# A one-core float32 transformer and recurrent block whose SBUF layout moves: a smaller GpSimd scratch, nine staging buffers in attention, fillers ahead of the column operands

## The chip, the cores and the metric

One core of a Trainium2 chip. The metric is device microseconds of one execution. The kernel before was timed three times: 881.23, 882.3 and 886.79 us, median 882.3 us. On 1 % of that, 8.8 us, rest the words faster, same and slower below.

## The reference

Two layers on one sequence of T = 256 tokens, D = 1024, everything float32 (cut):

```python
def first_block(x, mem, positions, ...):
    h = rms_norm(x, attn_norm_g)
    proj = h @ w_in                      # split into c_q, c_kv, k_pe, rq, rk, rv, rg
    a_out = mla_group(...)               # causal attention, 4 heads
    r_out = retention_group(...)         # chunked retention, 4 heads
    x = x + concat([a_out, r_out]) @ w_out
    x = x + memory_cross_attention(rms_norm(x, ...), rms_norm(mem, ...), ...)
    return x + hierarchical_moe(rms_norm(x, ...), ...)   # 32 experts, top 2

def hybrid_layer(x, p_i, ...):
    z = rmsnorm(x, g_mix) @ w_in         # 7 parts: RNN, convolutions, gates
    ...
    x = x + merged @ w_out
    g, u = split(rmsnorm(x, g_ffn) @ w_gate_up)
    x = x + (silu(g) * u) @ w_down
    return x + sigmoid(rmsnorm(x, g_ple) @ w_ple_gate) * (p_i @ w_ple)
```

## The kernel before, in words

All weights lie in one long array in the order of use, cut into chunks of mostly 128 x 2048 float32 (1 MB). `Stream.load` fetches them on one DMA queue of SyncE (L171), always in that order. There are three families: the A chunks (attention and cross attention), 96 M chunks for the experts (eight groups of four experts, in each eight gate/up chunks and four down chunks; they are numbered 0 to 95 here), and the B chunks (second layer).

**Columns.** Outside the experts a matrix product is done in columns: `dense_w` (L239) makes one 128x256 result from blocks of 128x128. For float32 accuracy a weight piece of 128x512 is first split: `wh` is a rounded copy of it (ScalarE, L195) and `wl` the remainder (VectorE, L196); an activation has likewise a high part and a low part (`hh` and `ll`; `ch`/`cl` and `moh`/`mol` in attention, `ach`/`acl`, `xch`/`xcl`, `pth`/`ptl` in cross attention). Each block then costs three matmuls of 256 columns: `wh` by high, `wh` by low, `wl` by high. `lead` (L249) does the same for several columns at once. `wh` and `wl` have four buffers up to the experts and eight after (WBUF_A, WBUF_B).

**Experts.** A chunk is used raw as moving operand (L1017 gate/up, L1068 down), and its buffer is free when TensorE has read it. While attention and cross attention still compute, M chunks are fetched ahead into whatever tiles are idle. Which one takes which chunk is written down by `_plan` from the list ORDER: three tiles "r", seven "rx" (RINGX), "ll" and "hh" (a ring of two each), four "w", "ck", "cv", two "rz" (RINGZ) and one "xs", 23 in all. So chunks 0 to 22 go out before the experts begin and chunk 23 takes the tile of chunk 0, and so on round. Each load waits on its tile alone, but the queue is strictly in order: an issue that waits holds up all that follow. In the last group fewer kinds of tiles are allowed, as those of the second layer take their place.

At group 4 (chunk 48) the program has a branch (L951, for experts with too many tokens; its body isn't run with these inputs). The tile "rz" is left out of the plan for the chunks before it, and its pool is released and opened again there.

**Second layer.** After the last group's scatter (L1054) the columns begin again at L239 with the B chunks in "w" and "r" tiles. They go on to the end.

**Addresses.** Every tile has a fixed place in each of the 128 partitions of SBUF; pools are stacked in the order of their allocation on top of the GpSimd scratch, and pools with side="right" grow from the other end. No operation of the kernel names an address; they follow from the sizes of what is allocated before.

Of the kernel before, what the change touches and what calls it, by code (L numbers as in the profile page):

```python
# [9 lines left out]
F32 = mybir.dt.float32  # L10
F32R = mybir.dt.float32r
I32 = mybir.dt.int32
BF16 = mybir.dt.bfloat16
# [5 lines left out]
P = 128  # L19
T = 256  # L20
D = 1024
KT = 8
EPS = 1e-6
NEG = -1e30
NE = 32
# [6 lines left out]
CHUNK = 2048  # L32
RING1 = 4
RING2 = 3
RINGX = 7
RINGZ = 2
WARM = 16
WBUF_A = 4
WBUF_B = 8
AHEAD = 3  # L40
# [68 lines left out]
def block_kernel(tc, wst, cst_d, csa_d, sml_d, rw_d, dec_d, xt_d, pt_d, pos_d, out_d, dbg=None):  # L109
    nc = tc.nc  # L110
    V, S, TE = nc.vector, nc.scalar, nc.tensor

    glob = tc.alloc_tile_pool(name="glob", bufs=1)
    smp = tc.alloc_tile_pool(name="smp", bufs=2)
    xsp = tc.alloc_tile_pool(name="xsp", bufs=1)
    hlp = tc.alloc_tile_pool(name="hlp", bufs=2)
    psd = tc.alloc_tile_pool(name="psd", bufs=4, space=PSUM)
    psa = tc.alloc_tile_pool(name="psa", bufs=3, space=PSUM)
    pss = tc.alloc_tile_pool(name="pss", bufs=1, space=PSUM)
    ring1 = tc.alloc_tile_pool(name="ring1", bufs=RING1)  # L120
    crs = tc.alloc_tile_pool(name="crs", bufs=1)
    wsp = tc.alloc_tile_pool(name="wsp", bufs=WBUF_A)

# [16 lines left out]

    ident, ones = C("ident"), C("ones")
    ltb = glob.tile([P, P], BF16, name="ltb")
    oneb = glob.tile([P, P], BF16, name="oneb")


    class Stream:
# [71 lines left out]
    ws = Stream()  # L218
# [146 lines left out]
    nc.sync.dma_start(x0[:, 4:8], xt_d[:, 4:8])  # L365
    ws.load(4)
    nc.sync.dma_start(cst, cst_d)
    csa = wsp.tile([P, NCSA], F32, name="csa", bufs=1)
    nc.sync.dma_start(csa, csa_d)
    nc.sync.dma_start(sml, sml_d)  # L370
    posi = rtmp.tile([P, T], I32, name="posi")
    nc.sync.dma_start(posi, pos_d)
# [23 lines left out]
    ch = mla.tile([P, 3, T], F32R, name="ch")  # L396
    cl = mla.tile([P, 3, T], F32R, name="cl")
    csq = rtmp.tile([P, 3, T], F32, name="csq")
    qsq = mla.tile([P, 6, T], F32, name="s6")
    ksq = mla.tile([P, 5, T], F32, name="s5")  # L400
    kpe = mla.tile([P, T], F32, name="kpe")
# [143 lines left out]
    V.tensor_copy(ltb, C("lt"))  # L545
    V.memset(oneb, 1.0)

    moh = mla.tile([P, KT, T], F32R, name="moh")
    mol = mla.tile([P, KT, T], F32R, name="mol")


    def softmax_pt(ps, nk, f, pool, ptd):
        mx = smp.tile([P, 1], F32, name="mx")
# [70 lines left out]

    bns = mla.tile([P, 8, 6], F32, name="bns")
    bna = mla.tile([P, 8, 2], F32, name="bna")
    ro = mla.tile([P, 8, P], F32, name="s6")

    def retention(h):
# [186 lines left out]
        V.tensor_mul(m.rearrange("p t (g e) -> p (t g) e", g=4), o, gsb)  # L816

    rps = psa.tile([P, 3, NE], F32, name="a")
    for i, mats in enumerate(((ltb,), (oneb, ltb), (oneb, oneb))):
        for j, mat in enumerate(mats):  # L820
            for k in range(2):
                TE.matmul(rps[:, i], mat, msk[k][:, j], start=j == 0 and k == 0, stop=j == len(mats) - 1 and k == 1)
# [89 lines left out]
    V.tensor_copy(gate[:, :, :, 4:5], r2[:, :, None, None].to_broadcast([P, 2, NGRP, 1]))  # L912

    lam = G("lam", 0, 8)
    na = smp.tile([P, 8], F32, name="na")
    with tc.issue_after(ins1.ins):
        V.tensor_scalar(na, lam, -1.0, None, op0=OP.mult)
    V.tensor_tensor(na, na, lam, op=OP.min)
    ee = smp.tile([P, 8], F32, name="ee")
    S.activation(ee, na, AF.Exp)  # L920
    den = smp.tile([P, 8], F32, name="den")
    V.tensor_scalar(den, ee, 2.0, None, op0=OP.add)
    V.reciprocal(den, den)
    s1 = smp.tile([P, 8], F32, name="s1")
    V.tensor_mul(s1, ee, den)
    s2 = smp.tile([P, 8], F32, name="s2")
    V.tensor_mul(s2, s1, s1)
    hq = smp.tile([P, 8], F32, name="hq")
    V.memset(hq, 1.0 / 19)
    for k in (17, 15, 13, 11, 9, 7, 5, 3, 1):  # L930
        V.tensor_mul(hq, hq, s2)
# [1 line left out]
    V.tensor_mul(hq, hq, s1)  # L933
    sp8 = glob.tile([P, 8], F32, name="sp8")
    spn = glob.tile([P, 8], F32, name="spn")
    mn = smp.tile([P, 8], F32, name="mn")
    with tc.issue_after(ins1.ins):
        V.tensor_scalar(mn, lam, -1.0, 0.0, op0=OP.mult, op1=OP.max)
    V.scalar_tensor_tensor(sp8, hq, 2.0, mn, op0=OP.mult, op1=OP.add)
# [6 lines left out]
    def overflow():  # L946

        n_it = nc.values_load(ntrip[0:1, 0:1], min_val=0, max_val=NGRP)
        wexp = wst[OFFS[NA]:OFFS[NA + NM]].rearrange("(g c p f) -> g c p f", g=NGRP, c=12, p=P)
        lpp = tc.alloc_tile_pool(name="lpp", bufs=1, side="right")  # L950
        with tc.If(n_it > 0):  # L951
            with tc.For_i(0, n_it, 1) as gi:
                gres = lpp.tile([P, 2, NE], F32, name="gres")
                V.tensor_scalar(gres, rank, float(CAP - RBASE), None, op0=OP.is_ge)
                for tt in range(2):
                    gv = gres[:, tt].rearrange("p (g e) -> p g e", g=NGRP)
                    V.tensor_mul(gv, gv, gate[:, tt, :, 0:4])
                    V.tensor_scalar(gres[:, tt], gres[:, tt], r2[:, tt:tt + 1], None, op0=OP.mult)
                xg = lpp.tile([P, KT, T], F32, name="lxg")
                for kt in range(KT):  # L960
                    pt = small()
                    for tt in range(2):
                        TE.transpose(pt[:, tt], xt[:, tt, kt * P:(kt + 1) * P], ident)
                    V.tensor_copy(xg[:, kt].rearrange("p (t c) -> p t c", t=2), pt)
                for q in range(4):
                    pg = [bank() for _ in range(2)]
                    for kt in range(KT):
                        w = lpp.tile([P, 512], F32, name="lw", bufs=2)
                        nc.gpsimd.dma_start(w, wexp[bass.ds(gi, 1), kt, :, q * 512:(q + 1) * 512]
                                          .rearrange("a p f -> p (a f)"))  # L970
                        for tt in range(2):
                            TE.matmul(pg[tt], xg[:, kt, tt * P:(tt + 1) * P], w, start=kt == 0, stop=kt == KT - 1)
                    at = lpp.tile([P, 2, T], F32, name="lat")
                    for tt in range(2):
                        a = lpp.tile([P, T], F32, name="la")
                        S.activation(a, pg[tt][:, 0:T], AF.Silu, scale=r2[:, tt:tt + 1])
                        V.scalar_tensor_tensor(a, pg[tt][:, T:512], gres[:, tt, bass.ds(gi * 4 + q, 1)], a,
                                               op0=OP.mult, op1=OP.mult)
                        pt = small()
                        for f in range(2):  # L980
                            TE.transpose(pt[:, f], a[:, f * P:(f + 1) * P], ident)
                        V.tensor_copy(at[:, :, tt * P:(tt + 1) * P], pt)
                    for hf in range(2):
                        wd = []
                        for f in range(2):
                            w = lpp.tile([P, 512], F32, name="lw", bufs=2)
                            nc.gpsimd.dma_start(w, wexp[bass.ds(gi, 1), 8 + 2 * hf + f, :, q * 512:(q + 1) * 512]
                                              .rearrange("a p f -> p (a f)"))
                            wd.append(w)
                        for m in range(4):  # L990
                            for f in range(2):
                                TE.matmul(acc[4 * hf + m], wd[f][:, m * P:(m + 1) * P], at[:, f], start=False, stop=False,
                                          skip_group_check=True)
        lpp.release()
# [332 lines left out]
            eng = nc.sync if m % 4 == 0 else nc.scalar  # L1327
            eng.dma_start(out_d[:, a:m + 1], x6[:, a:m + 1])

    for pool in (ft, fp, wsp, ws.pools["r2"], pss, psa, psd, ring1, hlp, xsp, smp, glob):  # L1330
        pool.release()


# [199 lines left out]
```

## Time and profile before

| what | before |
|---|---|
| median of 3 runs | 882.3 us (881.23 to 886.79) |
| profiled execution, its own time | 881.19 us |
| its span | 879.5 us |
| granted TensorE clock over the span | 0.987 |
| TensorE busy | 834.5 us, 95 % |
| VectorE busy | 558.1 us, 63 % |
| ScalarE busy | 460.5 us, 52 % |
| weights read | 212.70 MB, 243 GB/s over the span |

The profiled execution lies 1.1 us below the median. Of its 881.19 us, 1.7 us lie around the span. The page's busy time of a matmul counts from its start to a modelled end, and neighbours overlap in it; how fast matmuls follow each other is read from their number in a stretch without a pause.

### The profile page before, as it was taken

The page shows a single profiled execution, that of the slowest core. Times are in us where ns is not written, and L with a number is a line of the kernel's source. Part 1 is how long each engine was busy: PE and PEld are TensorE (multiplying, and loading weights), DVE is VectorE, ACT ScalarE, POOL GpSimd, SP SyncE. Part 2 cuts the span into 40 slices and gives each one's busy share as a digit, 9 for nine tenths or more (in the row PEclk, how much of TensorE's full clock was granted, in tenths as well). Part 3 has the DMA queues.
Part 4 walks back from the last instruction along what each step waited for, and adds up shares of the span by engine and source line. Part 5 has one row for each costly group of instructions (what it writes and reads, how often), then busy time and mean ns, then how long its engine had stood idle before and what let it go on. Part 6 is the DMA issues. An engine that isn't in the chain of part 4 may idle for free.

```text
span 879.5 us, 16760 instructions
## 1 busy us (share of the span) xinstructions
PE 834.5 (95%) x6508; PEld 720.2 (82%) x6508; DVE 558.1 (63%) x1445; ACT 460.5 (52%) x947; POOL 3.0 (0%) x9
## 2 busy tenths in 40 slices
PE   8999999999999998699879999999999999999995
PEld 7898997998875443254349999999999999999995
DVE  6799768877663111111069959767987777766675
ACT  7787565664412111011056778687766555555563
POOL 0000000000000000000000000000000000000000
PEclk9999999999999999899899999999999999999998
DMA  8263544579779999999997536545545555553401
GB/s 327 97 230 133 186 160 144 192 304 397 274 292 392 424 426 421 423 423 424 426 424 278 208 139 219 201 180 199 214 175 193 192 192 183 179 178 134 141 4 48
DMA packets 32677, 214.89 MB, mean 244 GB/s; under 512 B 3792, under 2 KB 4688, under 8 KB 8272
## 3 DMA queue, kind: packets, MB, share of 16 engines
q1 hardware_dynamic: 31680, 212.05, 62.5%
q8 instruction: 53, 0.87, 0.4%
q0 software_dynamic: 336, 1.05, 0.3%
q10 hardware_dynamic: 576, 0.66, 0.2%
q14 instruction: 32, 0.26, 0.1%
HBM read 212.70 MB, written 1.05 MB: 243 GB/s over the span
## 4 chain that ended last, share of the span: by engine, by line
PE 76%; DMA 11%; DVE 6%; ACT 5%; issue 2%; DVEq 0%; ACTq 0%; SPq 0%
PE d L239 55%; DMA r<-wst 4%; PE a L1017 3%; DMA ll<-wst 2%; DMA w<-wst 2%; DMA rz<-wst 2%; PE a L1068 2%; PE d L1054 2%; PE a L851 2%; PE d L249 1%; ACT wh L195 1%; DVE wl L196 1%; PE st L851 1%; PE d L268 1%; PE d L269 1%
## 5 line engine op out<-in xcount | busy, mean ns | idle before, releaser
L239 PE MATMUL d<-hh,wl 128*128 128x256 f32 x1208 | 340.4, 282 | 1.4 <-DVE wl L196 1.4
L239 PE MATMUL d<-hh,wh 128*128 128x256 f32 x1208 | 340.4, 282 | 0.5 <-ACT wh L195 0.5
L239 PE MATMUL d<-ll,wh 128*128 128x256 f32 x1208 | 338.0, 280 | 0.0
L195 ACT ACTIVATE wh<-w 128x512 fp32r<-128x512 f32 (+1 forms) x291 | 180.2, 627 | 133.3 <-PE d L239 103.3
L196 DVE TENSOR_TENSOR wl<-w,wh 128x512 fp32r<-128x512 f32 (+1 forms) x291 | 197.6, 686 | 60.9 <-ACT wh L195 58.0
L239 PEld LDWEIGHTS d<-hh,wl 128*128 128x128 f32 x1208 | 227.0, 188 | 2.9 <-DVE wl L196 2.5
L239 PEld LDWEIGHTS d<-hh,wh 128*128 128x128 f32 x1208 | 227.0, 188 | 1.9 <-ACT wh L195 1.2
L239 PEld LDWEIGHTS d<-ll,wh 128*128 128x128 f32 x1208 | 227.3, 188 | 1.2 <-issue 1.0
L195 ACT ACTIVATE wh<-r 128x512 fp32r<-128x512 f32 (+1 forms) x126 | 77.4, 624 | 53.0 <-PE d L239 48.5
L196 DVE TENSOR_TENSOR wl<-r,wh 128x512 fp32r<-128x512 f32 (+1 forms) x126 | 84.8, 682 | 29.0 <-ACT wh L195 26.6
L239 PE MATMUL d<-ach,wl 128*128 128x256 f32 x176 | 49.5, 281 | 0.0
L239 PE MATMUL d<-ach,wh 128*128 128x256 f32 x176 | 49.3, 280 | 0.0
L239 PE MATMUL d<-acl,wh 128*128 128x256 f32 x176 | 48.9, 278 | 0.0
L1077 DVE COPY y<-a 128x256 f32<-128x256 f32 x16 | 6.8, 424 | 60.6 <-ACT y L1076 60.6
L1034 ACT ACTIVATE ss_acc<-a,gsl 128x256 f32<-128x256 f32 x8 | 3.8, 473 | 76.1 <-DVE gsl L1024 37.3
L1054 PEld LDWEIGHTS d<-ss_sq,y 128*128 128x128 f32 x128 | 23.0, 190 | 15.2 <-ACT y L1076 6.5
L1054 PE MATMUL d<-ss_sq,y 128*128 128x256 f32 x128 | 31.6, 388 | 3.3 <-ACT y L1076 2.4
L239 PEld LDWEIGHTS d<-ach,wh 128*128 128x128 f32 x176 | 33.1, 188 | 0.0
L239 PEld LDWEIGHTS d<-acl,wh 128*128 128x128 f32 x176 | 33.1, 188 | 0.0
L239 PEld LDWEIGHTS d<-ach,wl 128*128 128x128 f32 x176 | 33.0, 188 | 0.0
L851 PEld LDWEIGHTS a<-ss_sq,xt 128*128 128x128 f32 x136 | 16.9, 191 | 15.4 <-issue 6.7
L851 PEld LDWEIGHTS st<-ss_sq,xt 128*128 128x128 f32 x120 | 14.9, 191 | 14.0 <-issue 7.5
(456 smaller groups left out, 1236.4 us busy)
## 6 DMA issues: line engine op xcount, KB each, us to landing
w<-wst SPq DMA_DIRECT2D x83, 1024.0 KB, 4.9
r<-wst SPq DMA_DIRECT2D x39, 1024.0 KB, 5.1
rx<-wst SPq DMA_DIRECT2D x28, 1024.0 KB, 18.0
ll<-wst SPq DMA_DIRECT2D x9, 1024.0 KB, 19.5
hh<-wst SPq DMA_DIRECT2D x9, 1024.0 KB, 19.5
rz<-wst SPq DMA_DIRECT2D x8, 1024.0 KB, 19.5
ck<-wst SPq DMA_DIRECT2D x5, 1024.0 KB, 19.6
cv<-wst SPq DMA_DIRECT2D x5, 1024.0 KB, 19.7
```

The costliest lines, as they stand in the source:

```text
L195: S.activation(wh[:, :n], src, AF.Copy)
L196: V.tensor_sub(wl[:, :n], src, wh[:, :n].bitcast(F32))
L239: TE.matmul(ps, a, b[:, kt], start=n == 0, stop=n == last)
L249: TE.matmul(ps, a, b[:, kt], start=i == 0 and j == 0, stop=i == len(kts) - 1 and j == 2)
L268: TE.matmul(pst[tt], l[:, kt, sl], wh, start=False, stop=False)
L269: TE.matmul(pst[tt], h[:, kt, sl], wl, start=False, stop=i == len(kts) - 1)
L851: TE.matmul(ps[:, j], xt[:, tt, kt * P:(kt + 1) * P], oneh[:, tt], start=tt == 0, stop=tt == 1)
L1017: TE.matmul(pg[32 * q:32 * q + 32], xgs[:, kt, 32 * q:32 * q + 32], w[:, 512 * q:512 * q + 512], start=kt == 0, stop=kt == KT - 1)
L1034: S.activation(a, pg[:, 0:T], AF.Silu, scale=gsl[:, 4:5])
L1054: mm = ins = TE.matmul(acc[m], y[:, m % 4 * P:(m % 4 + 1) * P], sc, start=False, stop=last, skip_group_check=True)
L1068: ins = TE.matmul(py[32 * q:32 * q + 32], at[:, f, 32 * q:32 * q + 32], w[:, 512 * q:512 * q + 512], start=f == 0, stop=f == 1)
L1077: V.tensor_copy(y[:, 256:512], py[:, 256:512])
```

## The change

It sets the scratch of GpSimd's DMA descriptors from its standard 16,384 bytes per partition to 1,024, and with what comes free it has two more "rx" tiles and one "rz" fewer (24 in ORDER in place of 23). Three fillers (`even`, `edge`, `meven`), a wider `csa` and an earlier place for `moh`/`mol` move the addresses. The constant matrix `oneb` is kept as one column and broadcast, seven small tiles go from pool `smp` to `rtp`, and two tiles of the branch's body take the names of others.

```diff
-RINGX = 7
-RINGZ = 2
+RINGX = 9
+RINGZ = 1
+EDGE = 248
+EVEN = 104
...
     xsp = tc.alloc_tile_pool(name="xsp", bufs=1)
+    smp.tile([P, EVEN], F32, name="even", bufs=1)
     hlp = tc.alloc_tile_pool(name="hlp", bufs=2)
...
     ring1 = tc.alloc_tile_pool(name="ring1", bufs=RING1)
+    edge = tc.alloc_tile_pool(name="edge", bufs=1, side="right")
+    edge.tile([P, EDGE], F32, name="edge")
...
-    oneb = glob.tile([P, P], BF16, name="oneb")
+    oneb = glob.tile([P, 1], BF16, name="oneb")
...
-    csa = wsp.tile([P, NCSA], F32, name="csa", bufs=1)
-    nc.sync.dma_start(csa, csa_d)
+    csa = wsp.tile([P, 480], F32, name="csa", bufs=1)
+    nc.sync.dma_start(csa[:, 0:NCSA], csa_d)
...
     csq = rtmp.tile([P, 3, T], F32, name="csq")
+    moh = mla.tile([P, KT, T], F32R, name="moh")
+    mol = mla.tile([P, KT, T], F32R, name="mol")
     qsq = mla.tile([P, 6, T], F32, name="s6")
...
-    moh = mla.tile([P, KT, T], F32R, name="moh")
-    mol = mla.tile([P, KT, T], F32R, name="mol")
...
+    mla.tile([P, 16], F32, name="meven")
...
-    for i, mats in enumerate(((ltb,), (oneb, ltb), (oneb, oneb))):
+    ob = oneb.to_broadcast([P, P])
+    for i, mats in enumerate(((ltb,), (ob, ltb), (ob, ob))):
...
-    na = smp.tile([P, 8], F32, name="na")
+    na = rtp.tile([P, 8], F32, name="na")
...
-                gres = lpp.tile([P, 2, NE], F32, name="gres")
+                gres = smp.tile([P, 2, NE], F32, name="ss_sq")
...
-                        a = lpp.tile([P, T], F32, name="la")
+                        a = smp.tile([P, T], F32, name="ss_acc")
...
-    for pool in (ft, fp, wsp, ws.pools["r2"], pss, psa, psd, ring1, hlp, xsp, smp, glob):
+    for pool in (ft, fp, wsp, ws.pools["r2"], pss, psa, psd, ring1, hlp, xsp, smp, glob, edge):
...
-    nc = bacc.Bacc("TRN2", target_bir_lowering=False, num_devices=1)
+    nc = bacc.Bacc("TRN2", target_bir_lowering=False, num_devices=1, dynamic_dma_scratch_size=1024)
```

What the layouts give, as the remainder of a tile's start address in a partition by 512 bytes (read from the two built programs; the buffers of a ring all have the remainder shown):

| tiles | before | after |
|---|---|---|
| `hh`, `ll` | 256 | 0 |
| `wh`, `wl` up to the experts | 32 | 0 |
| `wh`, `wl` in the second layer | 480 | 0 |
| `ch`, `cl` | 32 | 0 |
| `moh`, `mol` | 224 | 0 |
| `ach`/`acl`, `xch`/`xcl`, `pth`/`ptl` | 256 | 0 |
| weight tiles `w`, `ck`, `cv`, `xs` | 256 | 0 |
| weight tiles `r`, `rx` | 480 | 0 |
| weight tile `rz` | 448 | 416 |

The order of instructions on TensorE, VectorE and ScalarE is the same in both but for buffer names in the experts and the place of one small memset. What moves is SyncE's order of loads. In cross attention, where M chunks 3 to 9 of before are issued into "rx" (the number behind a name tells single tiles of a ring apart), SyncE has before:

```order
45 L171 DMA w_3110<-wst 128x2048
46 L171 DMA rx<-wst 128x2048 x2
47 L171 DMA w_3225<-wst 128x2048
48 L171 DMA rx<-wst 128x2048 x5
49 L171 DMA ll<-wst 128x2048
50 L171 DMA hh<-wst 128x2048
51 L171 DMA w_3460<-wst 128x2048
52 L171 DMA ck<-wst 128x2048
```

and after:

```order
45 L177 DMA w_3116<-wst 128x2048
46 L177 DMA rx<-wst 128x2048 x2
47 L177 DMA w_3231<-wst 128x2048
48 L177 DMA rx<-wst 128x2048 x7
49 L177 DMA ll<-wst 128x2048
50 L177 DMA hh<-wst 128x2048
51 L177 DMA w_3470<-wst 128x2048
52 L177 DMA ck<-wst 128x2048
```

Two loads more stand ahead of the first "ll". At the start of the experts, where the first turn of the list ends and the second begins with the "r" tiles, SyncE has before:

```order
57 L171 DMA ll<-wst 128x2048
58 L171 DMA hh<-wst 128x2048
59 L171 DMA rz<-wst 128x2048 x2
60 L171 DMA xs<-wst 128x2048
61 L171 DMA r_3820<-wst 128x2048
62 L171 DMA r_3838<-wst 128x2048
63 L171 DMA r_3844<-wst 128x2048
```

and after:

```order
57 L177 DMA ll<-wst 128x2048
58 L177 DMA hh<-wst 128x2048
59 L177 DMA rz<-wst 128x2048
60 L177 DMA xs<-wst 128x2048
61 L177 DMA r_3844<-wst 128x2048
62 L177 DMA r_3850<-wst 128x2048
63 L177 DMA r_3856<-wst 128x2048
```

One "rz" has gone, and the first "r" is chunk 24 in place of chunk 23. At the end of the experts, with the last eight M chunks and the first B chunks (512 and 1024 wide), SyncE has before:

```order
115 L171 DMA ll<-wst 128x2048
116 L171 DMA hh<-wst 128x2048
117 L171 DMA xs<-wst 128x2048
118 L171 DMA rz<-wst 128x2048 x2
119 L171 DMA ll<-wst 128x2048
120 L171 DMA hh<-wst 128x2048
121 L171 DMA ck<-wst 128x2048
122 L171 DMA cv<-wst 128x2048
123 L171 DMA r_4946<-wst 128x512
124 L171 DMA r_4952<-wst 128x512
125 L171 DMA r_4990<-wst 128x1024
```

and after:

```order
112 L177 DMA ll<-wst 128x2048
113 L177 DMA hh<-wst 128x2048
114 L177 DMA rz<-wst 128x2048
115 L177 DMA ll<-wst 128x2048
116 L177 DMA hh<-wst 128x2048
117 L177 DMA ck<-wst 128x2048
118 L177 DMA cv<-wst 128x2048
119 L177 DMA w_4952<-wst 128x512
120 L177 DMA w_4958<-wst 128x512
121 L177 DMA w_4996<-wst 128x1024
```

The last chunk still goes into "cv", and the first B chunks go into "w" tiles in place of "r" tiles.

## Rows read from the trace of the kernel before

**Rows 1.** The page: busy time by engine, causes of the chain, two groups of splits.

```profile
PE 834.5 (95%) x6508; PEld 720.2 (82%) x6508; DVE 558.1 (63%) x1445; ACT 460.5 (52%) x947; POOL 3.0 (0%) x9
...
PE 76%; DMA 11%; DVE 6%; ACT 5%; issue 2%; DVEq 0%; ACTq 0%; SPq 0%
...
L195 ACT ACTIVATE wh<-w 128x512 fp32r<-128x512 f32 (+1 forms) x291 | 180.2, 627 | 133.3 <-PE d L239 103.3
...
L195 ACT ACTIVATE wh<-r 128x512 fp32r<-128x512 f32 (+1 forms) x126 | 77.4, 624 | 53.0 <-PE d L239 48.5
```

**Rows 2.** Windows of L239: start:end, length, PE busy (count), PEld busy, PEclk, DMA share, GB/s.

```profile
0.00:252.00 252.00, 148.17 (x1128) 137.57 (x1128) 1.00 0.58 220
594.80:844.50 249.70, 242.37 (x2046) 241.18 (x2045) 1.00 0.49 175
0.00:880.00 880.00, 552.00 (x4536) 538.79 (x4536) 0.99 0.63 244
```

**Rows 3.** The same view, stretches in which L239 runs without a pause.

```profile
51.05:66.08 15.03, 15.03 (x129) 15.03 (x128) 1.00 0.58 215
155.00:175.00 20.00, 20.00 (x172) 20.00 (x172) 1.00 0.53 191
500.00:575.00 75.00, 75.00 (x645) 75.00 (x644) 1.00 0.54 194
660.00:750.00 90.00, 90.00 (x767) 90.00 (x766) 1.00 0.53 188
```

**Rows 4.** Timeline of PE at two places: start, length, engine, line, operation, count.

```profile
25.88 0.28 PE L239 MATMUL d<-ch,wl 128*128 128x256 f32 x1
...
26.35 0.28 PE L239 MATMUL d<-ch,wh 128*128 128x256 f32 x1
...
257.32 1.91 PE L380 MATMUL a<-cst 128*128 128x256 bf16 x16
```

**Rows 5.** Timeline of SyncE's queue, loads of M chunks: start, length over the group, load.

```profile
263.17 3.49 SPq L171 DMA_DIRECT2D r<-wst  x3
...
299.06 0.33 SPq L171 DMA_DIRECT2D hh<-wst  x1
...
316.13 15.29 SPq L171 DMA_DIRECT2D rx<-wst  x7
...
336.07 0.33 SPq L171 DMA_DIRECT2D hh<-wst  x1
...
346.04 5.32 SPq L171 DMA_DIRECT2D w<-wst  x3
```

**Rows 6.** Windows of all engines (PE, PEld, DVE, ACT, POOL busy), then PEclk, DMA share, GB/s.

```profile
227.60:251.00 23.40, 21.95 (x172) 20.64 (x172) 14.15 (x33) 10.28 (x23) 0.00 (x0) 1.00 0.59 221
...
270.00:450.80 180.80, 158.64 (x1126) 74.91 (x1122) 24.42 (x83) 23.44 (x58) 0.00 (x0) 0.95 1.01 423
431.00:442.00 11.00, 7.72 (x40) 0.92 (x40) 0.15 (x2) 0.00 (x0) 0.00 (x0) 0.69 1.01 429
```

**Rows 7.** DMA issues at 251.0, 263.2, 264.0, 431.2, and GpSimd's four: us to landing last.

```profile
ll<-wst SPq DMA_DIRECT2D x1, 1024.0 KB, 4.9
...
r<-wst SPq DMA_DIRECT2D x1, 1024.0 KB, 7.4
...
r<-wst SPq DMA_DIRECT2D x1, 1024.0 KB, 9.0
...
cv<-wst SPq DMA_DIRECT2D x1, 1024.0 KB, 19.7
...
decm<-dec POOLq DMA_DIRECT2D x4, 192.0 KB, 4.0
```

**Rows 8.** Timeline of PE in the last group of experts, with the wait before each.

```profile
426.72 3.02 PE L1017 MATMUL a<-w,xgs 128*32 128x512 f32 x24
...
441.01 1.07 PE L1017 MATMUL a<-rz,xgs 128*32 128x512 f32 x8 [0.69 <-DMA rz<-wst]
...
450.89 1.07 PE L1068 MATMUL a<-cv,ss_acc 128*32 128x512 f32 x8
```

More of the change, by code (lines that the diff above doesn't have):

```diff
@@ L918, in block_kernel @@
     V.tensor_tensor(na, na, lam, op=OP.min)
-    ee = smp.tile([P, 8], F32, name="ee")
+    ee = rtp.tile([P, 8], F32, name="ee")
     S.activation(ee, na, AF.Exp)
-    den = smp.tile([P, 8], F32, name="den")
+    den = rtp.tile([P, 8], F32, name="den")
     V.tensor_scalar(den, ee, 2.0, None, op0=OP.add)
     V.reciprocal(den, den)
-    s1 = smp.tile([P, 8], F32, name="s1")
+    s1 = rtp.tile([P, 8], F32, name="s1")
     V.tensor_mul(s1, ee, den)
-    s2 = smp.tile([P, 8], F32, name="s2")
+    s2 = rtp.tile([P, 8], F32, name="s2")
     V.tensor_mul(s2, s1, s1)
-    hq = smp.tile([P, 8], F32, name="hq")
+    hq = rtp.tile([P, 8], F32, name="hq")
     V.memset(hq, 1.0 / 19)
@@ L935, in block_kernel @@
     spn = glob.tile([P, 8], F32, name="spn")
-    mn = smp.tile([P, 8], F32, name="mn")
+    mn = rtp.tile([P, 8], F32, name="mn")
     with tc.issue_after(ins1.ins):
```

## The prediction, made before the changed kernel was run

> **What bounds the kernel now.** I read the page first: TensorE is busy for 834.5 us of 879.5, and 76 % of the chain that ended last is TensorE, 11 % DMA [rows 1]. So a change must either make matmuls follow each other faster or remove one of the places where TensorE waits for a load. The windows of L239 come next. They count 4536 of its column matmuls in the trace, 1128 of them before 252 us and 2046 between 594.8 and 844.5 us [rows 2]. Where they run without a pause, the distance of one start to the next is the length of the stretch divided by the count; as the last one's modelled end lies 0.28 us behind its start [rows 4], I add that to the length. The four stretches give 15.31/129 = 118.7 ns, 20.28/172 = 117.9, 75.28/645 = 116.7 and 90.28/767 = 117.7 [rows 3], all at a granted clock of 1.00, the 2.4 GHz level.
>
> The experts are different. Between 270 and 450.8 us the DMA engines are busy for 1.01 of the time [rows 6], while before, from 227.6 to 251 us, the share is 0.59. A 1 MB load takes 2.44 to 2.49 us (below), so this stage lasts as long as its loads. The end shows it: the last chunk is issued at 431.16 and lands 19.7 us later [rows 7], at 450.9, and TensorE's matmul on "cv" starts at 450.89 [rows 8]. An earlier landing of the last chunk is an earlier end of the stage, until TensorE itself is the bound.
>
> **The change part by part.**
>
> *Two more "rx", one fewer "rz".* The order rows of cross attention show two loads ahead of where "ll" stood. They fall into the stretch with a share of 0.59, which has 0.41 x 23.4 = 9.6 us idle; two loads need 4.9 us. They delay nothing that TensorE waits for there, if the queue's idle time is not just behind them; uncovered they would cost up to 4.9 us. At the start of the experts the first load that must wait for TensorE goes out at 263.17 [rows 5]; before, it is chunk 23, after, chunk 24. Before, chunk 23 takes 7.4 us, as loads lie ahead of it, and chunk 24, issued at 264.0, takes 9.0 [rows 7]: it lands at 273.0. After, one "rz" load fewer lies ahead, and the issue at 263.17 that now is chunk 24 finds the queue nearly empty. An empty queue needs 4.9 us (the "ll" of 251 us) [rows 7]: 268.1, a gain of 273.0 - 268.1 = 4.9 us. If it needs the 7.4 us of chunk 23 it lands at 270.6, a gain of 2.4. I take 4.9, since the load that has gone was just ahead. From there the queue is full in both kernels, so every later chunk keeps this lead.
>
> *Addresses of the weight tiles.* With eight loads in flight an issue waits for the landing eight before it, so distances of issues are distances of landings. From the "hh" issue at 299.06 to the first "rx" at 316.13 seven issues follow, released by landings in "w", "ck", "cv", "w", "w", "w" and "ll": 17.07/7 = 2.44 us each. From the "hh" at 336.07 to the last of the three "w" (346.04 + 5.32 - 0.33 = 351.03) six follow, released by six landings in "rx": 14.96/6 = 2.49 each [rows 5]. So tiles on a multiple of 256 bytes land at 2.44, those on 480 at 2.49. A turn of the list has 12 loads of 23 in "r", "rx" and "rz"; of the 72 chunks from 24 on, 35 land off a multiple before and three (in "rz") after: 32 x 0.05 = 1.6 us less. By bounds: nothing, if not the address but the place in the turn is the cause, and 72 x 0.05 = 3.6 us. Together with the lead 4.9 + 1.6 = 6.5 us, and the last chunk lands at 444.4.
>
> The Trainium skill ("DMA: Bandwidth & Descriptors", section on how a descriptor splits into AXI transactions) says that a transfer which doesn't start on a multiple of 256 bytes begins at the boundary below, and what it fetches in vain still costs. For a row of 8 KB this would be an estimate of 33 pieces in place of 32, 3.1 % or 0.08 us of 2.44; the rows have 0.05, and by the page's figure the sum would be about 1 us lower.
>
> *Can TensorE follow?* In the last group three gate/up chunks take 3.02 us when they don't wait, from 426.72 on; eight would be done at 426.72 + 8.05 = 434.8, and are done at 441.01 + 1.07 = 442.1 [rows 8]. So 7.3 us are to be had before TensorE bounds, more than 6.5. In that stretch the granted clock was 0.69 [rows 6] behind waits of half a microsecond and more; with the waits shorter it should stay up, and if it doesn't, the gain falls to some 4 us. The part's range is 2.4 + 0 to 7.3, taken at 6.5.
>
> *The columns.* Their operands move from remainders 32, 224, 256 and 480 to 0. The fastest pace seen is 116.7 ns. Were all at it, the 1128 before the experts would gain at most 2.0 ns each, 2.3 us (the 192 on "moh" only 1.2, so 2.1), and the 2046 after 594.8 us 1.0 ns, 2.0 us: 4.1 us. But stretches three and four have the same addresses and both paces, so that there something else than the address decides; between the two families the address of `wh` differs (32 and 480). I take the 2.1 us of the first family and nothing of the second. The bounds are wide: no gain at all, or, downward, the bf16 matmuls of 256 columns, whose 16 take 1.91 us, so (1.91 - 0.27)/15 = 109 ns [rows 4]; all columns at that would be 4536 x 8.3 ns, 38 us. I stay by the nearest rows, which are columns of the same type.
>
> *The split of weights.* Reading "w" (remainder 256) takes ScalarE 627 ns and "r" (480) 624 [rows 1]; the new remainder changes nothing here, taken at 0, bounded by +-3 ns for 417 splits, 1.3 us, and hidden beside TensorE.
>
> *Small scratch, broadcast, small tiles.* GpSimd issues five loads, four "decm" in retention with 4.0 us to landing [rows 7]. Nothing in the trace shows what its scratch holds; if one load had to wait for the one before it this might show once, so 0 to 4.0 us, taken at 0, as TensorE and VectorE have other work there. `oneb` as a broadcast column is read by six matmuls of some 0.1 us: 0, at most 0.5 us. The moved small tiles and the branch's body, which isn't run, cost 0.
>
> *Sum.* 881.2 - 6.5 - 2.1 = 872.6 us on the profiled execution. The three runs have 881.23, 882.3 and 886.79; from half way between the two nearest ones, 881.7, it is 873.1.
>
> **The rivals.**
>
> A. *The columns keep their pace*; only the loads gain. For it: remainders 32 and 256 of the moving operand both give columns near 117 to 118, and the pace switches with no address changed. Against it: the families differ. 881.7 - 6.5 = 875.2. The Trainium skill ("SBUF — State Buffer", specifications, and its box on cachelines) counts lines of 16 bytes alone; every remainder in question is a multiple of 16, so by that page 512 has no worth, and this rival holds. The rows speak half against it, with 118.7 against 116.7.
>
> B. *The columns fall below any pace seen*, because only a remainder of 0 for all operands lets reads go unhindered. For it: 116.7 ns lies above the 109 of bf16, and no column in this trace has all operands at 0. Against it: no remainder seen so far gave less than 116.7. At 114 ns, 4541 x 3.6 ns = 16 us: 859; at 115.2 some 864.
>
> C. *The gain of the loads doesn't come*: the two early loads push "ck", "cv" and "w" behind them, and these wait for a buffer as late as before, or the chain waits for TensorE in the middle. For it: a wait of the queue for one tile holds up all. Against it: 9.6 us of idle time. Then 881.7 - 1.6 = 880.1, or 878 with the columns' 2.1.
>
> D. *The slower side*: stationary and moving operand now begin at the same remainder in every column, and reading both at once may collide. For it: nowhere in the second layer do they do so before. Against it: `ch` and `wh` did, both at 32, and the four steps from 25.88 to 26.35 us are 117.5 ns each, with the rounding at most 120 [rows 4]. At 120 ns: 4541 x 2.4 = 10.9 us, 875.2 + 10.9 = 886.1. It decides from 6.5 us / 4541 = 1.4 ns on, at a mean of 119.0 ns; over 121.1 ns it is over 1 % slower.
>
> **How the numbers follow.** The forecast has a chance of 0.42 (its own range 869 to 876), A 0.20, B 0.15, C 0.13, D 0.10. A measurement of this kernel can tell about 1 %, 8.8 us: below 873.5 and above 891.1. Faster: 0.24 of the forecast's share, 0.06 of A's (a lead nearer 7.3 with some fewer bytes off the multiple), all 0.15 of B: 0.45. Slower: 0.06 of D. Within 1 %: the remaining 0.49. The range runs from 863 (B beyond 115 ns is left out, about 0.1) to 881 (D is left out).
>
> **What would show it.** Right: the first "r" load of the experts lands near 268, the last chunk near 444.4 and the "cv" matmul with it; the waits for "ll", "hh", "xs" and "rz" after 426 us shrink; and unbroken column stretches read 116.7 ns before 252 us and 116.7 to 117.7 behind. Wrong: a column pace under 116 ns or over 119 anywhere (B, D); landings of the last chunk unchanged (C); a wait for "decm" in retention.

## The result and the profile after

The changed kernel takes 887.92 us (median of 19 runs, 885.22 to 893.24); the kernel before, run beside it, 882.32 us (19 runs, 879.31 to 886.79). The ratio is 1.0066, 95 % interval 1.0051 to 1.008: slower by 5.6 us, inside the 1 % that I called no change, but on the other side of the forecast and above the range. The profiled execution has a span of 887.0 us where before had 879.5.

The page of the changed kernel, in the lines that answer to [rows 1]:

```profile
PE 843.5 (95%) x6508; PEld 733.4 (83%) x6508; DVE 559.0 (63%) x1445; ACT 461.6 (52%) x947; POOL 3.0 (0%) x9
...
PE 70%; DMA 18%; DVE 5%; ACT 4%; issue 2%; DVEq 0%; ACTq 0%; SPq 0%
...
L201 ACT ACTIVATE wh<-w 128x512 fp32r<-128x512 f32 (+1 forms) x292 | 180.5, 626 | 137.4 <-PE d L245 103.7
```

TensorE is busy 9 us longer for the same 6508 matmuls, and the split of weights costs what it did (626 ns from "w", before 627). The column line (L239 before, L245 now) in stretches without a pause, to be read as [rows 3] (length plus 0.28 us, divided by the count):

```profile
52.87:68.10 15.23, 15.23 (x128) 15.23 (x128) 1.00 0.60 208
155.10:177.90 22.80, 22.80 (x191) 22.80 (x191) 1.00 0.52 186
500.00:575.00 75.00, 75.00 (x627) 75.00 (x627) 1.00 0.53 185
660.00:750.00 90.00, 90.00 (x752) 90.00 (x751) 1.00 0.50 177
```

121.2 (the stretch's edges count most in the shortest one), 120.8, 120.1 and 120.1 ns, where [rows 3] had 118.7, 117.9, 116.7 and 117.7. From start to start inside these stretches it is 120.0 in all four. At full clock, then, each column matmul takes the same 120.0 ns.

The loads went the other way. SyncE's queue, at the places of [rows 5], and the landings, as in [rows 7]:

```profile
265.51 3.49 SPq L177 DMA_DIRECT2D r<-wst  x3
...
432.67 0.33 SPq L177 DMA_DIRECT2D cv<-wst  x1
```

```profile
r<-wst SPq DMA_DIRECT2D x1, 1024.0 KB, 5.3
...
cv<-wst SPq DMA_DIRECT2D x1, 1024.0 KB, 15.0
...
decm<-dec POOLq DMA_DIRECT2D x4, 192.0 KB, 4.6
```

The first load freed by TensorE, now chunk 24, lands 5.3 us after its issue, at 270.8; before, chunk 24 landed at 273.0. The last chunk lands at 432.67 + 15.0 = 447.7, before at 450.9. And the end of the experts, as [rows 8], with the same place of the kernel before in the second fence:

```profile
445.26 3.78 PE L1061 MATMUL d<-ss_sq,y 128*128 128x256 f32 x8 [0.56 <-ACT y L1083]
...
449.95 1.03 PE L1075 MATMUL a<-cv,ss_acc 128*32 128x512 f32 x8
...
454.89 0.39 PE L245 MATMUL d<-hh,wh 128*128 128x256 f32 x1
```

```profile
447.98 1.99 PE L1054 MATMUL d<-ss_sq,y 128*128 128x256 f32 x8 [0.57 <-ACT y L1076]
...
456.23 0.38 PE L239 MATMUL d<-hh,wh 128*128 128x256 f32 x1
```

The "cv" matmul no longer starts at the landing but 2.3 us behind it: the eight scatter matmuls ahead of it took 3.78 us in place of 1.99. Windows of all engines (columns as [rows 6]) of the changed kernel say why, and show one more thing at the start:

```profile
30.00:52.00 22.00, 20.04 (x101) 16.19 (x101) 18.06 (x94) 15.52 (x35) 0.00 (x0) 0.92 0.32 117
...
227.60:251.00 23.40, 21.49 (x168) 20.21 (x166) 14.76 (x34) 11.40 (x26) 0.00 (x0) 1.00 0.80 308
...
442.00:449.00 7.00, 5.78 (x24) 2.76 (x21) 2.05 (x6) 2.26 (x6) 0.00 (x0) 0.53 1.01 414
```

From 442 to 449 us the granted clock was 0.53, nearly the 1.2 GHz level throughout, behind waits that TensorE still had after 410 us, for loads and for VectorE (engine, line, what for; us in total, times, longest):

```profile
PE a L1024 <- DMA rz<-wst: 1.4, 1, 1.4
...
PE st L1048 <- DVE ss_acc L1042: 1.1, 1, 1.1
...
PE a L1075 <- DMA hh<-wst: 0.7, 1, 0.7
```

In the 11 us before that, still at a clock of 1.00, TensorE waited 2.4 us for loads and 1.6 us for VectorE.

From 30 to 52 us the clock was 0.92, where before had 1.00; by an estimate that is at most 22 x 0.08 = 1.8 us. Seven of the twelve kernels below, six of them with the fillers, had 1.00 in this window and five 0.84 to 0.92, and six had their first long column stretch begin at 51.2 to 51.6 us (before: 51.1), so I do not count it to the change. From 227.6 to 251 us the DMA share rose from 0.59 to 0.80: the two early loads did fall into idle time.

So the 7.5 us of the two spans divide thus. Up to the first freed issue 265.51 - 263.17 = +2.3 (up to 1.8 of them the clock). From there to the first column of the second layer 189.4 in place of 193.1 = -3.7. From there to the end 432.1 in place of 423.3 = +8.8. The last is the columns: 4536 - 1128 = 3408 of them lie behind the experts [rows 2]; from start to start their mean was 117.4 ns and is 120.0, and 3408 x 2.6 ns = 8.9 us.

### The profile page after: what moved, and what is told of

The parts are those of the page before. It is cut to its first block, busy times and chain, and to the rows that moved or that the text cites. A ratio compares the mean times of both kernels' runs of the same rounds, so it can differ in the third digit from the quotient of the medians.

```text
span 887.0 us, 16753 instructions
## 1 busy us (share of the span) xinstructions
PE 843.5 (95%) x6508; PEld 733.4 (83%) x6508; DVE 559.0 (63%) x1445; ACT 461.6 (52%) x947; POOL 3.0 (0%) x9
## 4 chain that ended last, share of the span: by engine, by line
PE 70%; DMA 18%; DVE 5%; ACT 4%; issue 2%; DVEq 0%; ACTq 0%; SPq 0%
PE d L245 56%; DMA rx<-wst 9%; DMA w<-wst 4%; DMA rz<-wst 2%; PE a L1024 2%; DMA r<-wst 2%; PE d L255 1%; ACT wh L201 1%; DVE wl L202 1%; PE d L274 1%; PE a L730 1%; PE d L273 1%; PE d L275 1%; PE a L751 1%; PE a L858 1%
## 5 line engine op out<-in xcount | busy, mean ns | idle before, releaser
L245 PE MATMUL d<-hh,wh 128*128 128x256 f32 x1208 | 343.8, 285 | 1.1 <-ACT wh L201 1.1
L245 PE MATMUL d<-hh,wl 128*128 128x256 f32 x1208 | 343.4, 285 | 1.0 <-DVE wl L202 0.9
L245 PE MATMUL d<-ll,wh 128*128 128x256 f32 x1208 | 342.4, 284 | 0.0
L245 PEld LDWEIGHTS d<-hh,wl 128*128 128x128 f32 x1208 | 231.4, 192 | 2.4 <-DVE wl L202 2.0
L245 PEld LDWEIGHTS d<-hh,wh 128*128 128x128 f32 x1208 | 231.2, 192 | 2.3 <-ACT wh L201 1.6
L245 PEld LDWEIGHTS d<-ll,wh 128*128 128x128 f32 x1208 | 231.5, 192 | 1.2 <-issue 1.0
L245 PE MATMUL d<-ach,wh 128*128 128x256 f32 x176 | 49.8, 283 | 0.0
L245 PE MATMUL d<-acl,wh 128*128 128x256 f32 x176 | 49.8, 283 | 0.0
L245 PE MATMUL d<-ach,wl 128*128 128x256 f32 x176 | 49.8, 283 | 0.0
L1061 PE MATMUL d<-ss_sq,y 128*128 128x256 f32 x128 | 33.4, 404 | 2.9 <-ACT y L1083 2.1
L245 PEld LDWEIGHTS d<-ach,wh 128*128 128x128 f32 x176 | 33.8, 192 | 0.0
L245 PEld LDWEIGHTS d<-acl,wh 128*128 128x128 f32 x176 | 33.8, 192 | 0.0
L245 PEld LDWEIGHTS d<-ach,wl 128*128 128x128 f32 x176 | 33.8, 192 | 0.0
```

The source lines that it names most:

```text
L245: TE.matmul(ps, a, b[:, kt], start=n == 0, stop=n == last)
L1061: mm = ins = TE.matmul(acc[m], y[:, m % 4 * P:(m % 4 + 1) * P], sc, start=False, stop=last, skip_group_check=True)
```

## The experiments

Theory D came out of the first four runs: the pace of a column goes by the difference between the start addresses of its weight (`wh`, `wl`, the stationary operand) and its activation (`hh` and its kin, the moving one), and a difference of 0 is a bad one (E, in the first expectations, is its special case: equal remainders by 512 are slow). Rivals: the weight's own address (S), the activation's own (M), or no address at all (N). In the fences of this section the columns are those of [rows 2], of the column line alone; each pace in the text is (length + 0.28)/count of the row shown, unless it is called start to start, which is the mean over the distances inside one unbroken stretch.

**Rings and fillers apart.** The first kernel is the one before with only

```diff
-RINGX = 7
-RINGZ = 2
+RINGX = 9
+RINGZ = 1
...
+    nc = bacc.Bacc("TRN2", target_bir_lowering=False, num_devices=1, dynamic_dma_scratch_size=1024)
```

and the two tiles of the branch's body under other names; the second is the changed one with `RINGX = 7`, `RINGZ = 2`.

> The kernel before with only the small scratch, nine rx and one rz (and the two tiles of the branch's body under other names, so that it fits); every operand of the columns keeps the remainder by 512 that it had before. All theories: columns stay at 116.7 to 118.4 ns, the columns begin again behind the experts earlier. Theory that the lead of the loads is real: the issue freed by TensorE at 263.2 lands near 268.1, the last chunk 4.9 us earlier than before (near 446), and the kernel takes 881.2 - 4.9 = 876.3 us or up to 2 us less. Rival: the gain is lost to TensorE at the end of the experts (clock and waits); then the last chunk is early but columns begin at most 2 us earlier and the kernel takes 879 to 880 us.

> The changed kernel with seven rx and two rz as before, all fillers kept. If the columns' 120.0 ns cause the loss, this kernel is slower than the changed one by what the rings gave (3.7 us between the first r load and the columns' new start): about 891 to 893 us, and every column stretch reads 120.0 ns. Rival, that the nine buffers bring the loss (by their place in SBUF or by traffic beside the columns): this kernel is near 880 us and the columns read under 118.4 ns.

The first took 878.67 us (before beside it 881.85; ratio 0.9958, interval 0.993 to 0.9987), the second 892.47 (1.0113, 1.0049 to 1.0178). With the two others this is a square: the rings give -3.2 without fillers and -4.6 with them, the fillers +10.6 and +9.2. So the loss does not come from the rings. The square is not exact: the first kernel has the small scratch as well, and the second has, beside the fillers, the rest of the change. That the addresses make the loss is read from the columns, here and in the experiments below. The first kernel's columns, and its landings (chunk 24, then the last):

```profile
154.00:175.00 21.00, 21.00 (x188) 21.00 (x187) 1.00 0.54 190
500.00:575.00 75.00, 75.00 (x645) 75.00 (x645) 1.00 0.55 197
660.00:750.00 90.00, 90.00 (x767) 90.00 (x766) 1.00 0.52 188
```

```profile
r<-wst SPq DMA_DIRECT2D x1, 1024.0 KB, 4.8
...
cv<-wst SPq DMA_DIRECT2D x1, 1024.0 KB, 16.0
```

Chunk 24 lands 4.8 us after its issue at 263.89, the last chunk (issued at 430.91) at 446.9: 4.0 us earlier than before, and the columns begin again at 453.34, 2.9 earlier. So both theories had a part: the lead is real, and TensorE's end of the experts gives about 1 us of it back. The "moh" columns surprise: 113.2 ns, with the remainders of the kernel before, where they took 117.9 [rows 3]. One difference can have two paces. The second kernel's columns:

```profile
500.00:575.00 75.00, 75.00 (x627) 75.00 (x626) 1.00 0.55 193
670.00:760.00 90.00, 90.00 (x752) 90.00 (x751) 1.00 0.50 181
```

120.1 in both: nine buffers have no part in it.

**A shift of everything, and a scan.** `EVEN = 40` in place of 104, and buffers for `wh` and `wl` of 2112 bytes:

```diff
-            wh = self.wsp.tile([P, UNIT], F32R, name="wh")
+            wh = self.wsp.tile([P, UNIT + 16], F32R, name="wh")
```

> The changed kernel with the first filler 256 bytes shorter: the activations (hh, ll, ach, xch, pth) and, up to the experts, wh and wl too start at remainder 256; in the second layer wh and wl stay at 0. Theory E (a column is slow where weight and activation start at the same remainder by 512): 120 ns before 252 us (256 and 256), under 118.4 ns after 455 us (0 and 256). Theory S (slow where the weight, the stationary operand, starts at 0): under 118.4 before, 120 after. Theory M (slow where the activation, the moving operand, starts at 0): under 118.4 in both. Theory N (the address has no part in it): 120 in both.

> The changed kernel with wh and wl buffers of 2112 bytes in place of 2048: in the second layer the eight buffers start at remainders 0, 64, 128, ... 448, with hh and ll at 0; each block of columns takes the next buffer after 12 matmuls. Theory E or S: only the buffer at 0 gives 120 ns, the mean over a stretch falls to about 117.5. Theory M: every buffer gives 120 ns. A finer rule (so many lines shared by the two) shows as a pace that changes with the buffer.

```profile
51.62:66.73 15.11, 15.11 (x128) 15.11 (x127) 1.00 0.60 210
...
500.00:575.00 75.00, 75.00 (x627) 75.00 (x626) 1.00 0.54 195
```

The shift changed nothing: 120.0 start to start in both families. In the second layer weight and activation had 0 and 256, so the slow case is not equality by 512 (theory E); what stays is a difference of 0 modulo 256, a weight or an activation at a multiple of 256, or N. The kernel's 885.3 us is one run. The scan rules out N:

```profile
500.00:575.00 75.00, 75.00 (x649) 75.00 (x648) 1.00 0.55 197
660.00:750.00 90.00, 90.00 (x778) 90.00 (x777) 1.00 0.53 191
```

Its mean is 116.0 and 116.0, and block by block the eight buffers repeat turn after turn. They do not follow each other in the order of their addresses. Put beside the addresses in the built program, the paces from start to start are, in order of time:

| `wh` at | `wl` at | ns |
|---|---|---|
| 192 | 192 | 113.3 |
| 448 | 448 | 113.7 |
| 384 | 384 | 117.9 |
| 320 | 64 | 113.4 |
| 64 | 320 | 113.3 |
| 256 | 128 | 119.0 |
| 128 | 256 | 118.2 |
| 0 | 0 | 119.4 |

So the block with a difference of 0 is the slowest, near the 120.0 that it has alone, and those whose difference is 64 or 192 modulo 256 are the fastest. This is the finer rule of the expectation: the pace changes with the buffer. The expectations for 192 and 320 further down took the buffers in the order of time for the order of addresses. The 119.0 that they give to 320 belongs to the buffer at 256 with `wl` at 128; the one at 320 had 113.4. A block of 12 columns can still carry something over from its neighbours. It took 876.5 us.

**One operand shifted by 32 bytes.** `EDGE = 240` moves the weights of the second layer (and "moh") by +32, `EVEN = 96` moves the activations "hh" by -32.

> The changed kernel with the filler at the right end 32 bytes shorter: in the second layer wh and wl (and r, rx) start at remainder 32, hh and ll stay at 0; before the experts wh, wl and hh stay at 0 and only ch and moh move to 32. Theory D (120 ns where the remainders of weight and activation differ by a multiple of 256): under 118.4 ns after 455 us, 120 in the hh columns of 50 to 75 us, under 118.4 in the moh columns of 155 to 177 us. Theory S (120 ns where the weight starts at a multiple of 256, whatever the activation): under 118.4 after 455 us, 120 in all columns before. Theory M (the activation alone): 120 after 455 us, under 118.4 in the moh columns. Theory N: 120 everywhere.

> The changed kernel with the first filler 32 bytes shorter: hh and ll start at remainder 480; wh and wl start at 480 before the experts and at 0 in the second layer; moh stays at 0. Theory D: 120 ns in the hh columns of 50 to 75 us (480 and 480), under 118.4 after 455 us (0 and 480) and in the moh columns (480 and 0). Theory S: under 118.4 in all columns before the experts, 120 after 455 us. Theory M: under 118.4 in the hh columns of both, 120 in the moh columns.

The first kernel ("moh", then two stretches of the second layer):

```profile
154.00:175.50 21.50, 21.50 (x186) 21.50 (x185) 1.00 0.51 186
500.00:575.00 75.00, 75.00 (x636) 75.00 (x635) 1.00 0.54 190
660.00:750.00 90.00, 90.00 (x763) 90.00 (x762) 1.00 0.53 188
```

The second, with its "hh" columns before the experts first:

```profile
51.34:66.57 15.23, 15.23 (x129) 15.23 (x128) 1.00 0.60 209
154.00:175.50 21.50, 21.50 (x187) 21.50 (x186) 1.00 0.55 186
500.00:575.00 75.00, 75.00 (x636) 75.00 (x635) 1.00 0.54 195
660.00:750.00 90.00, 90.00 (x763) 90.00 (x762) 1.00 0.52 184
```

Start to start, a weight at 32 with its activation at 0 and a weight at 0 with its activation at 480 both give 118.3 ns; "moh" with 0 and 32, and with 480 and 0, both give 116.7; weight and activation both at 480 give 119.9. Equal differences, equal pace, whichever operand was moved. S and M fall, and so does N. The kernel before fits in: up to the experts `wh` at 32 and `hh` at 256 are +32 modulo 256 and had 118.3; the second layer, 480 and 256, is -32 and had 116.7 or 117.8.

**Two larger shifts, and the modulus.** `EDGE = 200` (weights at +192 in the second layer), `EDGE = 168` (+320, that is +64), `EDGE = 224` (+96, and -96 for "moh").

> The changed kernel with the right filler 192 bytes shorter: in the second layer wh and wl start at remainder 192, hh at 0; ch and moh start at 192 too. In the scan the buffer at 192 had 113.4 ns. If that is a property of the remainders, all columns after 455 us take 113.3 to 114 ns (some 3456 x 6.3 ns = 22 us less than the changed kernel, about 866 us); if it hangs on what the blocks before it did (a rhythm of loads and reads that a stretch falls into), the stretch keeps one pace anywhere between 113 and 120 ns.

> The changed kernel with the right filler 320 bytes shorter: wh and wl of the second layer at remainder 320, hh at 0. In the scan the buffer at 320 had 119.0 ns. If the remainders settle the pace: 119 ns after 455 us, about 885 us. If the rhythm does, one pace for the whole stretch, not tied to 119.

> The changed kernel with the right filler 96 bytes shorter: in the second layer the weight starts 96 bytes behind the activation (96 and 0), in the moh columns 96 bytes ahead of it (0 and 96). So far +32 gave 118.3 ns, -32 gave 116.7 or 117.8, +64 and -64 gave 113.3 or 117.8, 0 and 256 gave 120.0. If the pace goes by the difference modulo 128, +96 is as -32 (116.7 or 117.8 after 455 us) and -96 as +32 (118.3 in the moh columns). If modulo 256 only, both are new values and need fit neither.

The kernels with 192 and with 320, one after the other:

```profile
500.00:575.00 75.00, 75.00 (x639) 75.00 (x638) 1.00 0.55 195
660.00:750.00 90.00, 90.00 (x797) 90.00 (x796) 1.00 0.56 198
```

```profile
500.00:575.00 75.00, 75.00 (x639) 75.00 (x638) 1.00 0.55 195
660.00:750.00 90.00, 90.00 (x796) 90.00 (x796) 1.00 0.54 190
```

117.8 ns in the first stretch and 113.3 in the second, in both, at unchanged addresses: a stretch falls into one of two rhythms and keeps it until something interrupts it. So the remainders do not settle the pace alone, as the first alternative had it, and 113.3, which the scan had at 192 and at 320, is one of the two. Nor do the higher parts of the addresses settle it: in the second stretch the activation changes from `hh` and `ll` to `ach` and `acl`, which lie more than 40 KB further on in the built program, at 771 us with 192 and at 769 us with 320, and the pace stays 113.3. The times were 874.0 and 871.9 us (one run each). The kernel with 96:

```profile
157.50:179.50 22.00, 22.00 (x185) 22.00 (x185) 1.00 0.54 190
505.00:580.00 75.00, 75.00 (x642) 75.00 (x641) 1.00 0.55 193
670.00:760.00 90.00, 90.00 (x761) 90.00 (x760) 1.00 0.51 183
```

117.3 and 118.6 at +96, 120.0 start to start at -96: not the values of -32 and +32, so 128 is not the modulus; 256 stands. Its 890.4 us can't be compared: its clock fell behind the experts and its long column stretch began at 471.7 us, some 8 us later than in the two others.

**Finer steps.** Here `wh` and `wl` lie shifted inside wider buffers of the second layer, by 16, 48, 80, 112 and 64 bytes in turn.

> The changed kernel with wh and wl of the second layer shifted inside wider buffers, by 16 bytes up to about 550 us, 48 to about 648, 80 to about 725, 112 to about 829, and 64 after that, hh at 0. If the pace depends on the difference in steps of 32 bytes (where the allocator puts tiles), 16 and 48 give 120.0 and 118.3 or 113 to 118; if finer steps count, new paces show, possibly one below 113.3 or one that holds in every stretch. No rival excludes either; before the experts all stays at 120.0 ns, and the second layer lies between 432 us (as in the changed kernel) and 410 us.

```profile
480.00:489.00 9.00, 9.00 (x79) 9.00 (x78) 1.00 0.68 243
564.00:594.00 30.00, 30.00 (x256) 30.00 (x255) 1.00 0.47 176
606.00:622.00 16.00, 16.00 (x132) 16.00 (x131) 1.00 0.47 171
670.00:720.00 50.00, 50.00 (x424) 50.00 (x423) 1.00 0.52 183
750.00:830.00 80.00, 80.00 (x669) 80.00 (x668) 1.00 0.45 158
855.00:873.00 18.00, 18.00 (x156) 18.00 (x155) 1.00 0.01 2
```

Start to start: +16 gives 118.3. +48, which begins at 551 us inside an unbroken stretch, gives 118.3 to the end of that stretch, and behind the next pause an alternation of 130 and 117 with a mean of 123.3 (the worst seen), so it has two paces too. +80 gives 118.8, +112 gives 120.0, and +64 117.8. In these stretches no step of 16 bytes beats 64; a step that was seen in one stretch alone may have a second pace. The kernel took 887.6 us.

**The version that follows.** All fillers stay, but csa is 16 floats wider, so that the first weights stand at 64, and a pad behind `wl` moves the weights of the second layer to -64 or to +64 (modulo 256) from `hh`:

```diff
-    csa = wsp.tile([P, 480], F32, name="csa", bufs=1)
+    csa = wsp.tile([P, 496], F32, name="csa", bufs=1)
...
     ws.after = []
+    wsp.tile([P, 16], F32, name="weven", bufs=1)
     rtp.release()
```

> The changed kernel with every column at a difference of 64 bytes or minus 64: csa 64 bytes wider (wh and wl of the first family at 64, hh, ch and moh at 0), and a pad of 64 bytes behind wh and wl of the second layer (448, hh at 0); rx and r stay at 0. By theory D with a rhythm: every stretch reads 113.3 or 117.8 ns, none 120.0; the time lies between 888 - 4656 x 2.2 ns = 877.7 us (all 117.8) and 888 - 4656 x 6.7 = 856.8 us (all 113.3), about 870 us where half the columns find the faster rhythm. By theory N it stays at 888.

> As the kernel with differences of 64 and minus 64, but with the second layer at plus 64 too (wh and wl at 320, hh at 0). By theory D with a rhythm, plus 64 and minus 64 have the same two paces, 113.3 and 117.8 ns, and the stretches fall into one or the other by what goes before; the only profile so far with plus 64 after 455 us had 113.3 in three stretches of five (871.9 us), the two with minus 64 had it in one stretch of six and in none. If plus 64 favours the faster rhythm, the fast runs lie near 865 to 872 us and 1.2 to 2 % under the kernel before; if the choice is free, they spread from 866 to 880 as those of the kernel with minus 64 did.

With -64 (the 16 above) it took 878.11 us (ten runs, 869.5 to 881.04; ratio 0.9927, 0.9892 to 0.9962), and in its profile all of the second layer had the slower rhythm:

```profile
500.00:575.00 75.00, 75.00 (x639) 75.00 (x638) 1.00 0.54 195
660.00:750.00 90.00, 90.00 (x766) 90.00 (x765) 1.00 0.52 187
```

With +64 (a pad of 48 floats in place of 16) it took 868.69 us (six runs, 866.67 to 876.1; before beside it 882.32; ratio 0.9838, 0.9793 to 0.9883), and its profile has both rhythms:

```profile
500.00:575.00 75.00, 75.00 (x664) 75.00 (x663) 1.00 0.57 200
660.00:750.00 90.00, 90.00 (x766) 90.00 (x765) 1.00 0.53 188
```

113.4 and 117.9. It beats both kernels, and the intervals of +64 and -64 do not overlap. In the two profiles with +64 behind the experts (320 above, and this one) four of six long stretches had 113.3 each, in the two with -64 one of six and none. The runs of -64 spread over 11.5 us, those of the kernel before beside them over 6.1 (879.81 to 885.9). A choice of rhythm made anew in each run would do that; but the changed kernel, with one pace everywhere, spreads over 8.0 us too, and only one run of each kernel has a profile, so this is not shown, nor whether +64 truly favours the faster rhythm. What tips a stretch into one or the other stays open. A short wait is enough: in the profile with -64 two longer steps (0.18 and 0.23 us) at 60.3 us part columns of 113.3 ns from columns of 117.8 ns, with the same activation and the same difference on both sides.

## Why the prediction was wrong

*The columns* is the step that failed. I took -2.1 us; the runs have +8.8 behind the experts and, by the estimate above, some +0.5 before them (the 2.3 us less the clock's 1.8). The reasoning had two faults. First, "stretches three and four have the same addresses and both paces, so that there something else than the address decides": the runs show that one difference allows two rhythms, so two paces at one address do not clear the address. Second, I looked for the best remainder of each operand, where the runs show that the two operands' difference counts: +32 and -32 in the kernel before (118.3; 116.7 or 117.8), 0 in the changed one (120.0). Laying all operands on one grid made every difference the same bad one.

*Rival D* was the right one, with the right place, a mean of 120.0 ns as its price and a forecast of 886.1 us, and I gave it a tenth. What I held against it, four steps of 117.5 ns with `ch` and `wh` both at 32 [rows 4], was too little: four steps at the resolution of the timeline can't tell 117.5 from 120. The same trace has a longer stretch of such columns at another place:

```profile
21.79 0.28 PE L239 MATMUL d<-ch,wh 128*128 128x256 f32 x1
...
23.35 0.28 PE L239 MATMUL d<-cl,wh 128*128 128x256 f32 x1
```

These are 13 steps, and (23.35 - 21.79)/13 = 120.0 ns: the kernel before already showed D's pace at D's difference. That two reads collide, as D has it, is still not shown. (The rivals' sums count 4541 columns where [rows 2] has 4536; it changes no conclusion.) I should also have asked how the two families, +32 and -32, came to differ; that question leads to the difference.

*Rivals A and B*: the Trainium skill ("SBUF — State Buffer", specifications and the box on cachelines) counts lines of 16 bytes, by which no shift here should matter. The runs disagree, from 113.3 to 123.3 ns for the same matmul. B was not foolish: 113.3 exists, but at a difference of 64 or 192 and not at 0.

*The rings* came out in kind. The lead at chunk 24 was to be 4.9 us and is 9.85 - 5.3 = 4.5 from the freed issue on, 5.0 in the kernel with the rings alone; it was to survive to the end, and the last chunk lands 5.5 us sooner after that issue.

*The addresses of the weight tiles* were to give 1.6 us and give about 1.0 (71 landings in 176.9 us, before 177.8). The address is the cause and not the place in the turn, for the shifted kernels turn the two kinds round. The median distance of landings in "rx" is 2.49 us with the tiles at 480 (before) or at 32 (`EDGE = 240`) and 2.44 with them at 0 (changed, `EVEN = 96`); that in "ll" is 2.44 at 256 (before) and at 0 (changed), and 2.49 at 480 (`EVEN = 96`). The sum, 6.5, was 5.5 at the landing.

*Can TensorE follow?* was answered too kindly: of 5.5 us the columns' new start got 3.7, since the clock fell again, to 0.53, on the waits that were left, some of them for VectorE. I had priced such a fall at "some 4 us" in all, which is what was measured.

*Small scratch, broadcast, small tiles*: nothing seen. The four "decm" loads take 4.6 us to landing (4.0 before), but 3.9 to 4.8 in the twelve other kernels, all of which have the small scratch, and GpSimd waits for the same releasers as before.

## What to carry to other kernels

A filler that aligns all operands can be the wrong one: what counted here was how far the weight of a matmul starts from its activation, modulo 256 bytes, so read the pace of an unbroken stretch, from start to start, and try one shift of one operand before aligning both. When a stretch shows two paces at one address, look for a rhythm, and judge an address by long stretches of one kind. And split a change that does two things into its two halves before explaining its sum: here one half was worth -0.4 % and the other +1.1 %.

## What the runs showed of the hardware

The pace of a column matmul (weight 128x128, 256 columns, tiles of type float32r), at full clock and with the next weight load under it, by the difference of start addresses (weight minus activation, modulo 256 bytes):

| difference | ns from start to start | seen in |
|---|---|---|
| 0 | 120.0 | changed kernel, all stretches |
| 16 | 118.3 | finer steps |
| 32 | 118.3 | before (first family), two shifted kernels |
| 48 | 118.3 or 123.3 | finer steps |
| 64 | 113.3 or 117.8 | seven kernels, before ("moh") among them |
| 80 | 118.8 | finer steps |
| 96 | 117.3 or 118.7 | one kernel |
| 112 | 120.0 | finer steps |
| 128 | 117.9 | scan, blocks of 12 columns |
| 160 | 120.0 | one kernel |
| 192 | 113.3 or 117.8 | three kernels |
| 224 | 116.7 or 117.8 | before (second layer), two shifted kernels |

That the read of the next weight and the read of the activation get in each other's way would explain a dependence on their distance and a rhythm that locks in; no counter of such conflicts was seen, so that is argued. Beside it: 1 MB loads into tiles off a multiple of 256 bytes landed 2.49 us apart and on it 2.44 (medians), and with a scratch of 1,024 bytes for GpSimd's descriptors no wait of TensorE for one of its five loads shows.
